# Paged ring, sums in dead blocks and parted VectorE operations in a Strassen kernel for a gated pooling and convolution block

## The chip, the cores and the metric

One core of a Trainium2 chip runs the whole kernel. The metric is the device time of one execution in microseconds (us); the kernel before has a median of 2375.99 us over three runs.

## The reference

A decoder block on x of 256 tokens by 4096 channels, float32. Nearly all of its work is in the projections.

```
h = rmsnorm(x, norm_w)
proj = einsum('bsd,de->bse', h, w_in)              # 4096 -> 20480
u_p, z_p, u_c, b_c, c_c, z_c, g_logit = split(proj)
y_pool = causal_multiscale_pool(u_p, pool_w, pool_scale) * silu(z_p)
y_conv = causal_gated_shortconv(u_c, b_c, c_c, conv_w, conv_b) * silu(z_c)
br = einsum('bsnc,ncd->bsnd', stack([y_pool, y_conv]), w_branch)   # 2048 -> 4096, twice
merged = sum(sigmoid(g_logit + gate_b) * br)
x = x + einsum('bsd,de->bse', merged, w_out)       # 4096 -> 4096
out = rmsnorm(x, final_norm_w)
```

The pool means windows of 2, 4, 8 and 16 tokens by group and maps each group by a 512 x 512 matrix; the convolution has three taps.

## The kernel before, in words

**Units and steps.** An output block of 256 tokens by 1024 columns is a unit. In order: cu0, cc0, cz0, cb0 and cu1 to cb1 (convolution branch, `conv_units`, line 687), pz0, pu0, pz1, pu1 (pool branch), eight gates g0_0, g1_0 to g1_3, eight branch units b0_0, b1_0 to b1_3, four output units o0 to o3. A unit sums over its contraction in steps of 256 rows: 16 steps, in the b units 8. Each step reads one raw weight block of 128 partitions by 2048 numbers, 1 MB.

**Three products.** A number is split into a high part that float32r holds and a low rest, and a product of two is high*high + high*low + low*high: three matmuls of 128 x 128 by 128 x 512. A plain step (P) is eight products, 24 matmuls. A Strassen step (S, Winograd's form) is seven, 21 matmuls, but it needs sums of the weight block's quarters q0 to q3 (`Step.micros`, line 254): T1 and T3 = q0 + q1 and q0 + q2 in V, then V's first half + q2, and that + q3, in W. Of the activations the operands stand in `arena` with their splits, some in Strassen form.

**Who does what.** SyncE loads raw blocks, three buffers in turn (`issue_load`, line 1189). ScalarE copies a piece into the ring as float32r (`act`, line 68), VectorE subtracts to get the low part (`sub`, line 80). TensorE multiplies from the ring (`multiply`, line 1287). All VectorE operations on two tensors have the helper's line 72, all ScalarE ones 69, all step matmuls 1292. Some sums are helped: SyncE loads q0 twice into E, and GpSimd's queue adds q1 and q2 by an accumulating DMA (`move_add`, line 93), so that VectorE has no V to make; `HELPED` (line 624) lists the steps.

**The ring.** 62 pieces of 256 numbers a partition (`Ring`, line 205). A step takes contiguous blocks: 8 and 8 for P, 12, 8 and 8 for S; a block that does not fit before the end goes to the start. Space is given back in the order of its taking.

**What sets the order.** Each engine's instructions keep the order in which the program puts them in. `pump` (line 1214) runs after each group of matmuls: it puts in the next load when the block three before is split (`split`, set in `direct`, line 302), and the preparation of steps up to three ahead while the ring has room. `tick` (line 1280) runs once in six matmuls and takes an item of the unit's epilogue from `queue`, then a phase of a fill (`pop_fill`, line 959). Fills make the operands of the b and o units from y_d and m_d in device memory (stages sa, sb and, for a time, Y), in the last x unit g1_3, the first b units and o0. A Strassen operand's fill is four sums on VectorE (`sums_s`), a split on ScalarE (arena<-sa) and one on VectorE. Unit ends evacuate banks (E<-sums, `evacuate`, line 446). `PLACES` and `OUT` (lines 625 and 855) say which steps of a unit are S; pz1 and g0_0 hold also the band and mixing steps of the pool (`insert`, line 1006).

Of the kernel before, what the change touches and what calls it, by code (L numbers as in the profile page):

```python
# [42 lines left out]
NP_X, NS_X = 7, 9  # L43
NB = 2
NP_Y, NS_Y = (6, 5), (2, 3)
RING = 62
# [5 lines left out]
PACE = 5  # L52
TAIL = 3
# [3 lines left out]
def hybrid_block(ctx: ExitStack, tc: tile.TileContext, x, x_t, norm_t, w_first, w_in, pool_w, pool_scale,  # L57
# [48 lines left out]
    ring = sb("ring", [P, RING * KB], F32R)  # L106
# [4 lines left out]
    W = sb("W", [P, 2, NH])  # L111
# [7 lines left out]
    ossq = sb("ossq", [P, 2, 6])  # L119

# [48 lines left out]
    diag, ones, std = (op.tile([P, P], F32, name=n) for n in ("diag", "ones", "std"))  # L169
    rbc = op.tile([P, T], F32, name="rbc")  # L170
# [20 lines left out]
    class Operand:  # L191


        def __init__(self, kind, view, region):
            self.kind, self.view, self.region = kind, view, region
            self.ready = False

        def block(self, part, i):

            return self.view[:, part, i]  # L200
# [4 lines left out]
    class Ring:  # L205


        def __init__(self, size):
            self.size, self.head, self.live = size, 0, []

        def alloc(self, n):
            at = self.head if self.head + n <= self.size else 0
            for a, m, _, _ in self.live:
                if at < a + m and a < at + n:
                    return None
            if at == 0 and self.head + n > self.size and any(a >= self.head for a, *_ in self.live):
                return None
            block = [at, n, 0, n]
            self.live.append(block)
            self.head = at + n  # L220
            return block

        def release(self, block, n):
            block[2] += n
            while self.live and self.live[0][2]:
                first = self.live[0]
                first[0] += first[2]
                first[1] -= first[2]
                first[2] = 0
                if first[1]:  # L230
                    break
                self.live.pop(0)

    rg = Ring(RING)

    def piece(block, off, n):
        o = (block[0] + off) * KB
        return ring[:, o:o + n * KB]


    def place_of_sum(i):

        return (E, R)[i // 2][:, i % 2].rearrange("p (i n) -> p i n", i=2)


    class Step:
# [7 lines left out]
        def micros(self):  # L254
# [3 lines left out]
            def half(n):  # L258
                def f(block):
                    self.blocks[n] = block  # L260
                    self.h[n] = piece(block, 0, 4).rearrange("p (k n) -> p k n", k=2)
                    self.l[n] = piece(block, 4, 4).rearrange("p (k n) -> p k n", k=2)
                    q = r.rearrange("p (k n) -> p k n", k=2)[:, :, n * NH:(n + 1) * NH]
                    if self is steps[0] and n == 0:

                        act(self.h[n][:, 0], q[:, 0])
                        x_direct(0)
                        for k in range(2):
                            if k:
                                act(self.h[n][:, k], q[:, k])  # L270
                            sub(self.l[n][:, k], q[:, k], self.h[n][:, k].bitcast(F32))
                        return
                    if self is steps[0]:
                        for k in range(2):
                            act(self.h[n][:, k], q[:, k])
                            sub(self.l[n][:, k], q[:, k], self.h[n][:, k].bitcast(F32))
                        return
                    act(self.h[n], q)
                    sub(self.l[n], q, self.h[n].bitcast(F32))
                return f  # L280

            if self.kind == "P":
                self.blocks, self.h, self.l = [None] * 2, [None] * 2, [None] * 2
                return self.pre + [(8, None, half(0)), (8, None, half(1))] + self.post
            if self.kind == "S":
# [5 lines left out]
                def sums(_):  # L291
                    add(V, q[:, 0:1].to_broadcast([P, 2, NH]), q[:, 1:3])
# [1292 lines left out]
```

## Time and profile before

| what | value |
|---|---|
| runs, median (lowest to highest) | 2375.99 us (2373.97 to 2376.92), n 3 |
| profiled execution, first to last instruction | 2371.9 us |
| TensorE busy, matmuls | 2353.5 us, 10483 records |
| VectorE busy, instructions | 2176.7 us, 2234 |
| ScalarE busy, instructions | 1419.7 us, 1474 |
| DMA | 605.60 MB, mean 255 GB/s |
| granted TensorE clock | 0.999 |

The profiled execution has no time of its own beside the span; what lies around its first and last instruction is in the runs' times only. Times in rows are us from the span's start. A row of the order of time gives start, duration, engine, line, operation, out<-in and count; rows of equal work that follow each other are merged, and in brackets stands how long the engine was idle before, and for whom. A matmul's row is 0.39 us long though the next one starts sooner, since they are pipelined. A row of waits gives the waiting engine, the one waited for, the total in us, how often, and the longest. A row of groups gives count, busy us, mean ns of one, then the idle time before.

### The profile page before, as it was taken

To read this page: it belongs to the slowest core of one execution; us is meant where nothing else is said; L and a number is where in the kernel's file an instruction comes from. 1 tells how busy PE (TensorE), PEld (TensorE's weight loads), DVE (VectorE), ACT (ScalarE), POOL (GpSimd) and SP (SyncE) were. 2 spreads that over 40 slices of the span, in tenths; PEclk is the share of its full clock that TensorE was granted. 3 is DMA by queue.
4 is the path that set the end of the run, shared out by engine and by line. 5 is a ranking of instruction groups with operands and counts; after the bars stand their busy time and mean duration, and the time that the engine had idled before them with its cause. 6 is when DMAs were issued, how large, how long until landed. Compare 5 with 4: busy or idle time off the path is not lost.

```text
span 2371.9 us, 28071 instructions
## 1 busy us (share of the span) xinstructions
PE 2353.5 (99%) x10483; PEld 1946.2 (82%) x10483; DVE 2176.7 (92%) x2234; ACT 1419.7 (60%) x1474; POOL 134.5 (6%) x201
## 2 busy tenths in 40 slices
PE   9999999999999999999999999999999999999998
PEld 7888888888888888888888888887878888878886
DVE  8999899989999989989999999988998898899898
ACT  7565565656555656566665656565664556566564
POOL 0000000000002001000000000001100001000000
PEclk9999999999999999999999999999999999999999
DMA  8578678886778658658887888789866667778867
GB/s 335 189 253 252 224 263 276 261 253 215 262 252 265 224 211 251 231 219 262 278 281 232 295 285 276 244 285 293 285 240 226 260 229 267 244 241 285 280 222 267
DMA packets 105257, 605.60 MB, mean 255 GB/s; under 512 B 11232, under 2 KB 11488, under 8 KB 43936
## 3 DMA queue, kind: packets, MB, share of 16 engines
q1 hardware_dynamic: 83216, 512.30, 59.5%
q0 software_dynamic: 21472, 90.45, 16.0%
q8 instruction: 82, 1.34, 0.2%
q10 hardware_dynamic: 432, 1.07, 0.1%
q14 instruction: 55, 0.45, 0.1%
HBM read 571.26 MB, written 25.17 MB: 251 GB/s over the span
## 4 chain that ended last, share of the span: by engine, by line
PE 90%; DVE 5%; DMA 2%; issue 2%; ACT 1%; SPq 0%; POOL 0%; DVEq 0%; ACTq 0%; POOLq 0%
PE sums L1292 66%; PE shared L1292 22%; DVE ring L72 2%; PE shared L804 1%; PE shared L528 1%; DVE W L72 1%; ACT ring L69 1%; DMA R<-in_gate_b_dram 1%; DMA E<-in_w_in_dram 1%; DVE R L72 0%; DMA raw<-in_w_in_dram 0%; DVE V L72 0%; DVE arena L72 0%; DMA raw<-in_w_out_dram 0%; DVE sa L72 0%
## 5 line engine op out<-in xcount | busy, mean ns | idle before, releaser
L1292 PE MATMUL sums<-ring,arena 128*128 128x512 f32 x7641 | 1806.5, 390 | 2.8 <-ACT E L69 2.4
L1292 PEld LDWEIGHTS sums<-ring,arena 128*128 128x128 f32 x7641 | 1431.6, 188 | 301.1 <-ACT E L69 3.3
L72 DVE TENSOR_TENSOR ring<-raw,ring 128x1024 fp32r<-128x1024 f32 (+2 forms) x695 | 942.4, 1382 | 101.8 <-ACT ring L69 97.7
L69 ACT ACTIVATE ring<-raw 128x1024 fp32r<-128x1024 f32 (+2 forms) x695 | 801.8, 1182 | 284.9 <-PE sums L1292 174.9
L1292 PE MATMUL shared<-ring,arena 128*128 128x512 f32 x2484 | 627.7, 389 | 3.6 <-DVE ring L72 3.6
L1292 PEld LDWEIGHTS shared<-ring,arena 128*128 128x128 f32 x2484 | 465.5, 188 | 102.9 <-DVE ring L72 6.0
L69 ACT ACTIVATE ring<-W 128x1024 fp32r<-128x1024 f32 x207 | 219.9, 1062 | 364.2 <-DVE W L72 302.9
L72 DVE TENSOR_TENSOR ring<-W,ring 128x1024 fp32r<-128x1024 f32 x207 | 253.9, 1226 | 23.1 <-ACT ring L69 11.8
L69 ACT ACTIVATE ring<-V 128x1024 fp32r<-128x1024 f32 x154 | 162.7, 1057 | 144.5 <-DVE V L72 119.9
L72 DVE TENSOR_TENSOR V<-raw 128x1024 f32<-128x1024 f32 x154 | 187.9, 1220 | 7.6 <-DMA raw<-in_w_in_dram 6.8
L72 DVE TENSOR_TENSOR ring<-V,ring 128x1024 fp32r<-128x1024 f32 x154 | 187.9, 1220 | 1.3 <-ACT ring L69 1.3
L72 DVE TENSOR_TENSOR W<-W,raw 128x512 f32<-128x512 f32 x207 | 141.9, 685 | 0.0
L72 DVE TENSOR_TENSOR W<-V,raw 128x512 f32<-128x512 f32 x154 | 106.6, 692 | 4.7
L94 POOL DMA_DIRECT2D E<-in_w_in_dram x47 | 41.1, 875 | 765.1 <-DMA E<-in_w_in_dram 322.7
L72 DVE TENSOR_TENSOR R<-R,E 128x1024 f32<-128x1024 f32 (+1 forms) x49 | 77.1, 1592 | 4.0 <-DMA R<-in_gate_b_dram 1.8
L72 DVE TENSOR_TENSOR ring<-E,ring 128x1024 fp32r<-128x1024 f32 x57 | 69.5, 1219 | 1.9 <-ACT ring L69 1.9
L69 ACT ACTIVATE ring<-E 128x1024 fp32r<-128x1024 f32 x57 | 59.7, 1047 | 6.7 <-PE sums L1292 3.7
L72 DVE TENSOR_TENSOR R<-R,shared 128x512 f32<-128x512 f32 x87 | 59.6, 685 | 2.7 <-ACT R L69 0.8
L69 ACT ACTIVATE arena<-sa 128x512 fp32r<-128x512 f32 (+2 forms) x48 | 25.2, 555 | 57.5 <-DVE sa L72 57.5
L69 ACT ACTIVATE E<-sums,rin 128x512 f32<-128x512 f32 x76 | 49.2, 682 | 15.7 <-PE sums L1292 15.7
L72 DVE TENSOR_TENSOR W<-E,raw 128x512 f32<-128x512 f32 x53 | 36.6, 691 | 12.8 <-issue 5.7
L72 DVE TENSOR_TENSOR arena<-sa,arena 128x512 fp32r<-128x512 f32 (+2 forms) x48 | 27.5, 600 | 3.5 <-ACT arena L69 3.5
(143 smaller groups left out, 560.0 us busy)
## 6 DMA issues: line engine op xcount, KB each, us to landing
raw<-in_w_in_dram SPq DMA_DIRECT2D x318, 1024.0 KB, 5.5
raw<-in_w_branch_dram SPq DMA_DIRECT2D x64, 1024.0 KB, 5.2
raw<-in_w_out_dram SPq DMA_DIRECT2D x64, 1024.0 KB, 5.9
E<-in_w_in_dram SPq DMA_DIRECT2D x47, 512.0 KB, 7.3
E<-in_w_in_dram POOLq DMA_DIRECT2D x47, 512.0 KB, 8.6
gates_d<-R POOLq DMA_DIRECT2D x8, 1024.0 KB, 12.0
R<-in_gate_b_dram POOLq DMA_DIRECT2D x7, 1024.0 KB, 12.0
R<-E POOLq DMA_DIRECT2D x4, 1024.0 KB, 9.4
```

Source lines behind the costliest of these rows:

```text
L69: return pin(nc.scalar.activation(dst, src, func, **kw))
L72: return pin(nc.vector.tensor_tensor(out=dst, in0=a, in1=b, op=op))
L94: return pin(nc.gpsimd.dma_start(dst, src, accum_op=ALU.add))
L528: pin(nc.tensor.transpose(shared(j)[:, i * T + t * P:i * T + (t + 1) * P], src[:, t, c:c + P], ident))
L804: pin(nc.tensor.matmul(o, a[:, k, ts], b[:, k], start=(k, i) == (0, 0), stop=(k, i) == (3, 2)))
L1292: pin(nc.tensor.matmul(ps, lhs, rhs, start=n == 0, stop=n == u.total[b] - 1))
```

## The change

**Pages.** The ring is 16 pages of 4 pieces (64 pieces), one page for a high and a low part of 512 numbers. A step takes single pages in circular order, P 2 and 2, S 3, 2 and 2; each page is given back by itself after its product. A piece that crosses the ring's end is split by two instructions on each engine (`parts_of`). In plain steps the matmuls of a bank come in threes, first row block first, instead of sixes.

**Sums over dead raw blocks.** W is gone. The third and fourth sums are written over q0 and q1 of the raw block itself, and the block counts as split only after their own split. That last split is put off (`late`): ScalarE's half is put in between the next step's first copy and VectorE's operation, VectorE's half after the next step's first VectorE operation.

```
@@ Step.micros, kind S
+                    if not helped:
+                        late_high()
+                        add(V, q[:, 0:1].to_broadcast([P, 2, NH]), q[:, 1:3])
+                        self.third = bool(late)
+                        late_low()
+                    else:
+                        self.third = True
+                    if self.third:
+                        add(q[:, 0], v[:, 0], q[:, 2])
...
-                    act(self.dh, q[:, 1:4])
-                    add(W[:, 0], v[:, 0], q[:, 2])
-                    sub(self.dl, q[:, 1:4], self.dh.bitcast(F32))
-                    add(W[:, 1], W[:, 0], q[:, 3])
-                    self.split = True
+                    split(block, q[:, 1:4])
+                    if not self.third:
+                        add(q[:, 0], v[:, 0], q[:, 2])
...
-                    act(self.h13, v)
-                    sub(self.l13, v, self.h13.bitcast(F32))
-                    self.summed = True
+                    split(block, v)
+                    add(q[:, 1], q[:, 0], q[:, 3])
+                    self.summed = now[0]
...
-                    act(self.h24, W)
-                    sub(self.l24, W, self.h24.bitcast(F32))
+                    def low_part():
+                        split_sub(block, q[:, 0:2])
+                        self.split = True
+                    late.append([self, lambda: split_act(block, q[:, 0:2]), low_part])
@@ new
+    def split(block, src):
+        split_act(block, src)
+        late_high()
+        split_sub(block, src)
+        late_low()
```

On VectorE, in o0, where its first two Strassen steps are prepared; V and W hold sums, E gates, Y the branch's part, raw a weight block. Before:

```order
L72 TENSOR_TENSOR R<-R,Y 128x1024
L72 TENSOR_TENSOR V<-raw 128x1024
L72 TENSOR_TENSOR W<-V,raw 128x512
L72 TENSOR_TENSOR ring<-raw,ring 128x3x512
L72 TENSOR_TENSOR W<-W,raw 128x512
L72 TENSOR_TENSOR ring<-V,ring 128x2x512
L72 TENSOR_TENSOR ring<-W,ring 128x2x512
L72 TENSOR_TENSOR V<-raw 128x1024
```

VectorE at the same place of the changed kernel, from the first Strassen step on:

```order
L75 TENSOR_TENSOR V<-raw 128x1024
L75 TENSOR_TENSOR ring<-raw,ring 128x3x512
L75 TENSOR_TENSOR raw<-V,raw 128x512
L75 TENSOR_TENSOR ring<-V,ring 128x2x512
L75 TENSOR_TENSOR raw<-raw 128x512
L75 TENSOR_TENSOR R<-R,E 128x1024
L75 TENSOR_TENSOR R<-R,Y 128x1024
L75 TENSOR_TENSOR R<-R,E 128x1024
L75 TENSOR_TENSOR R<-R,Y 128x1024
L75 TENSOR_TENSOR ring<-raw,ring 128x2x512
L75 TENSOR_TENSOR V<-raw 128x1024
```

No sum stands directly behind the one that it reads now. The last split (ring<-raw,ring 128x2x512), by which the raw block comes free, stands behind the four R operations of the merge, which stood ahead of the step before.

**The sequences.** `SEQUENCES` writes every unit's order by hand, 204 S steps in place of 207, among them:

```
-        "pz1": (3, 6, 8, 9, 10, 11, 12, 14, 15),
+ 'pz1': 'ppbpmmpssppssssppss'
-        "g1_3": (3, 6, 7, 9, 11, 13, 14),
+ 'g1_3': 'ppspspppspsspssp', 'b0': 'ppppppss', 'o0': 'pppppssssppspsps'
```

Before, b0 was PPPPPSPS and o0 PPPPPPSSPSSSPSPS. Two more x operands get Strassen forms, in a tile `more` that lives from g0_0 to the end of g0_3 (`room_for_more`). At the end of b0_0, VectorE before; sa<-sa are a fill's sums, arena<-sa and arena<-Y splits of fills:

```order
L72 TENSOR_TENSOR ring<-V,ring 128x2x512
L72 TENSOR_TENSOR ring<-W,ring 128x2x512
L72 TENSOR_TENSOR ring<-raw,ring 128x1024
L72 TENSOR_TENSOR arena<-Y,arena 128x512
L72 TENSOR_TENSOR ring<-raw,ring 128x1024 x2
L72 TENSOR_TENSOR sa<-sa 128x128 x4
L72 TENSOR_TENSOR ring<-raw,ring 128x1024
L72 TENSOR_TENSOR arena<-sa,arena 128x512
```

VectorE there in the changed kernel:

```order
L75 TENSOR_TENSOR ring<-V,ring 128x2x512
L75 TENSOR_TENSOR raw<-raw 128x512
L75 TENSOR_TENSOR arena<-Y,arena 128x512
L75 TENSOR_TENSOR ring<-raw,ring 128x2x512 x3
L75 TENSOR_TENSOR sa<-sa 128x128 x4
L75 TENSOR_TENSOR ring<-raw,ring 128x2x512 x2
L75 TENSOR_TENSOR arena<-sa,arena 128x512
```

One split of a plain half-step has moved from before the fill's sums to behind them.

**More places for helped sums.** E and R have two each, and the fill's stage sa is a fifth while no fill uses it. `HELPED` is gone: any Strassen step may be helped, if a place is free when its load is two to five loads ahead (`LATEST` 2, `LEAD` 5; before 0 and 3). A helped step loads only q1 to q3 of its raw block. 68 steps are helped in place of 53.

```
-            if helped and helped[0].host is running[0] and sums_from[0] is not None and now[0] >= sums_from[0] and (
-                    helped[0].load_index < state["nl"] + LEAD):
+            if helped and helped[0].load_index < state["nl"] + LEAD:
                 t = helped[0]
-                at = next((i for i in t.slots if sums_in[i] is None or sums_in[i].summed), None)
+                at = next((i for i in t.slots if (in_sa(t) if i == 4 else t.host is running[0] and
+                           sums_from[i // 2] is not None and now[0] >= sums_from[i // 2])
+                           and (sums_in[i] is None or sums_in[i].summed and now[0] >= sums_in[i].summed + SETTLED)), None)
+        elif s.slot is not None:
+            load(r[:, NH:4 * NH], s.src.rearrange("p k n -> p (k n)")[:, NH:4 * NH])
@@ Fill.fetch
-            move(flat(st), self.src)
+            load(flat(st), self.src)
```

The last pair of lines moves the fills' fetches from GpSimd's queue to SyncE's. GpSimd's queue in g1_3 before; 128x1024 into E are the adding DMAs:

```order
L94 DMA E<-in_w_in_dram 128x1024
L91 DMA sb<-y_d 128x512
L94 DMA E<-in_w_in_dram 128x1024
L91 DMA sa<-y_d 128x512
L91 DMA gates_d<-R 128x2048
L91 DMA Y<-y_d 128x512
L91 DMA sb<-y_d 128x512
```

SyncE's queue there in the changed kernel, where 128x2x512 into E is the first half of a helped sum:

```order
L90 DMA sb<-y_d 128x512
L90 DMA raw<-in_w_in_dram 128x2048
L90 DMA E<-in_w_in_dram 128x2x512 x2
L90 DMA sa<-y_d 128x512
L90 DMA raw<-in_w_in_dram 128x2048
L90 DMA Y<-y_d 128x512
L90 DMA sb<-y_d 128x512
L90 DMA raw<-in_w_in_dram 128x2048 x2
L90 DMA sa<-y_d 128x512
L90 DMA Y<-y_d 128x512
L90 DMA raw<-in_w_in_dram 128x1536 x2
```

The fetches of y_d stand between weight loads now, and the halves of both sums are asked for with three loads still before the two raw blocks (128x1536) that they belong to.

390 lines of the change are left out of this document (202 added, 188 removed), and 17 rows, old and new, of the table PLACES.

## The prediction

> **What bounds the kernel now.** I read the page's head first, then the tensor engine's waits, then the order of time at the places where it waited.
>
> ```profile
> span 2371.9 us, 28071 instructions
> PE 2353.5 (99%) x10483; PEld 1946.2 (82%) x10483; DVE 2176.7 (92%) x2234; ACT 1419.7 (60%) x1474; POOL 134.5 (6%) x201
> PE shared L1292 <- DVE ring L72: 3.6, 4, 1.3
> PE sums L1292 <- ACT E L69: 2.4, 2, 2.1
> PE shared L1059 <- DVE rout L1064: 1.1, 1, 1.1
> PE sums L1292 <- DVE ring L72: 0.4, 2, 0.2
> ```
>
> The second line says that the matmuls fill the span; the waits, in all 7.5 us, are the whole of what a better order could win, and 1.1 of them belong to the start. A busy tensor engine could still be a slow one, so I took its pace from rows of merged matmuls:
>
> ```profile
> 1715.35 8.32 PE L1292 MATMUL sums<-ring,arena 128*128 128x512 f32 x36
> 1723.51 2.88 PE L1292 MATMUL shared<-ring,arena 128*128 128x512 f32 x12
> 1728.47 4.83 PE L1292 MATMUL sums<-ring,arena 128*128 128x512 f32 x20 [2.08 <-ACT E L69]
> 1725.95 1.04 ACT L69 ACTIVATE arena<-sa 128x512 fp32r<-128x512 f32 x2 [2.72 <-DVE sa L72]
> 1726.90 1.04 ACT L69 ACTIVATE ring<-raw 128x1024 fp32r<-128x1024 f32 x1
> 1727.85 1.56 ACT L69 ACTIVATE E<-sums 128x512 f32<-128x512 f32 x3
> ```
>
> Thirty-six matmuls take 8.32 us and twelve take 2.88: (8.32 - 2.88) / 24 = 0.2267 us each, whichever step they belong to. So time is the count of matmuls times 0.2267, plus waits. The wait shown is the passage from b0_0 to b1_0: the twelfth matmul of the second row starts at 1723.51 + 11 x 0.2267 = 1726.00, the next at 1728.47, so 2.47 - 0.23 = 2.2 us are lost. Its cause stands on ScalarE: the bank's evacuation (E<-sums) stood behind a fill's split (arena<-sa), which waited 2.72 us for VectorE. The same reckoning at the other places:
>
> ```profile
> 927.30 2.43 PE L1292 MATMUL sums<-ring,arena 128*128 128x512 f32 x10
> 929.97 0.74 PE L1292 MATMUL sums<-ring,arena 128*128 128x512 f32 x2 [0.24 <-DVE ring L72]
> 1645.49 0.39 PE L1292 MATMUL shared<-ring,arena 128*128 128x512 f32 x1
> 1647.17 0.73 PE L1292 MATMUL shared<-ring,arena 128*128 128x512 f32 x2 [1.30 <-DVE ring L72]
> 1649.13 0.39 PE L1292 MATMUL shared<-ring,arena 128*128 128x512 f32 x1
> 1649.98 2.11 PE L1292 MATMUL shared<-ring,arena 128*128 128x512 f32 x8 [0.47 <-DVE ring L72]
> 2087.57 0.50 PE L1292 MATMUL shared<-ring,arena 128*128 128x512 f32 x1
> 2089.37 0.72 PE L1292 MATMUL shared<-ring,arena 128*128 128x512 f32 x2 [1.29 <-DVE ring L72]
> 2091.32 0.40 PE L1292 MATMUL shared<-ring,arena 128*128 128x512 f32 x1
> 2092.24 2.12 PE L1292 MATMUL shared<-ring,arena 128*128 128x512 f32 x8 [0.53 <-DVE ring L72]
> ```
>
> From start to start less 0.23: pz1 loses 0.4 at 929 (929.97 less 927.30 + 9 x 0.2267, less 0.23); g1_3 loses 1.45 + 0.62, with some 0.3 in the longer rows, 2.4; o0 loses 1.57 + 0.69 and some 0.2, 2.5. With the 2.2 above that is 7.5 us in four places. In all but one, VectorE's split into the ring came last. Its load by stage:
>
> ```profile
> 1113.00:1193.90 80.90, 80.90 (x358) 67.00 (x357) 76.31 (x72) 50.17 (x48) 4.90 (x6) 1.00 0.79 258
> 1598.50:1683.40 84.90, 83.14 (x364) 67.78 (x364) 73.99 (x82) 48.98 (x53) 10.43 (x16) 1.00 0.87 285
> 2028.40:2115.30 86.90, 85.08 (x381) 69.57 (x380) 78.83 (x101) 52.49 (x64) 3.18 (x4) 1.00 0.72 233
> ```
>
> After a stretch's length come the busy times of the tensor engine, its weight loads, VectorE, ScalarE and GpSimd, then clock, DMA share and GB/s. The tensor engine works 80.90 of 80.90 us in g1_0, but 83.14 of 84.90 in g1_3 and 85.08 of 86.90 in o0. VectorE is no fuller in the two stages that lose time; it was held up there itself, and ran late. The granted clock is 1.00 in all three.
>
> **The change part by part.** The sequences put 204 Strassen steps where 207 were. Such a step is 21 matmuls, a plain one 24: 9 more, 9 x 0.2267 = **+2.0 us**, on the path with nothing to hide them. The new order inside plain steps (three matmuls on a bank, then the next) costs nothing: Strassen groups of three already run at 0.2267.
>
> VectorE next:
>
> ```profile
> L72 DVE TENSOR_TENSOR ring<-raw,ring 128x1536 fp32r<-128x1536 f32 x207 | 363.2, 1755 | 24.4 <-ACT ring L69 22.5 <-PE sums L1292 0.7
> L72 DVE TENSOR_TENSOR ring<-W,ring 128x1024 fp32r<-128x1024 f32 x207 | 253.9, 1226 | 23.1 <-ACT ring L69 11.8
> L72 DVE TENSOR_TENSOR V<-raw 128x1024 f32<-128x1024 f32 x154 | 187.9, 1220 | 7.6 <-DMA raw<-in_w_in_dram 6.8 <-DMA raw<-in_w_out_dram 0.8
> L72 DVE TENSOR_TENSOR W<-W,raw 128x512 f32<-128x512 f32 x207 | 141.9, 685 | 0.0
> 2047.88 1.22 DVE L72 TENSOR_TENSOR V<-raw 128x1024 f32<-128x1024 f32 x1
> 2049.13 0.69 DVE L72 TENSOR_TENSOR W<-V,raw 128x512 f32<-128x512 f32 x1
> 2049.74 1.75 DVE L72 TENSOR_TENSOR ring<-raw,ring 128x1536 fp32r<-128x1536 f32 x1
> 2051.41 0.69 DVE L72 TENSOR_TENSOR W<-W,raw 128x512 f32<-128x512 f32 x1
> ```
>
> An operation that reads its neighbour's result starts after its end (2049.13 against 2047.88 + 1.22, 0.03 later); one that doesn't starts 0.08 before it (2049.74 against 2049.82). Parting them is worth 0.11 us a pair. A step with its sums on VectorE was 1.22 + 0.69 + 1.755 + 0.685 + 1.22 + 1.226 = 6.8, with the last split waiting for ScalarE's copy of a W just made; I take 0.3 off each of 204, 61 us. Sums made by DMA go from 53 to 68 steps: 15 x 1.22 = 18 off. Three steps from Strassen (6.8) to plain (2 x 1.22): 13 off. Against that, blocks that wrap are split in two (0.685 twice for 1.22, with 0.08 of overlap: 0.08 each, some 60, 5 us), and two more operands get Strassen forms, some 4 us each. Net 61 + 18 + 13 - 5 - 8 = 79, 3 to 4% of 2176.7. None of that is time of the kernel: VectorE is covered by the ring's lead except at the four places.
>
> The Trainium skill speaks against this part: its page "VectorE: DVE Perf Modes", section "The DRAIN you can't avoid", has the next operation wait until the pipe is empty, whether or not a semaphore stands between. By it parting wins nothing and 61 us leave the sum above. The rows here disagree, since independent neighbours overlap by 0.08; no run has yet shown the parted order.
>
> At the places:
>
> - g1_3, 2.4 us lost. What held VectorE:
>
> ```profile
> 1623.12 0.87 POOL L94 DMA_DIRECT2D E<-in_w_in_dram  x1 [8.69 <-DMA E<-in_w_in_dram]
> 1623.66 0.89 POOL L91 DMA_DIRECT2D sb<-y_d  x1
> 1632.64 0.69 DVE L72 TENSOR_TENSOR W<-E,raw 128x512 f32<-128x512 f32 x1 [5.73 <-issue]
> ```
>
> The adding DMA left at 1623.12 and VectorE stood 5.73 us for its sum. The profile names no releaser for that wait; the sum in E is what the operation reads, and its DMA was the last to be issued. A sum is now asked for two to five loads ahead instead of none to three; fills of the operands leave by SyncE's queue, no longer behind the 8.69 us in which GpSimd's stood. Two loads earlier is two steps, 42 x 0.2267 = 9.5 us at least, over the 5.73. I take off 1.9 and leave 0.5 (bounds: 0 to 2.4 left). The page "DMA: Bandwidth & Descriptors" of the Trainium skill, section "Issuing engines are not separate DMA queues", says that another issuing engine saves only issue time; by it the move to SyncE brings nothing, and the earlier request alone would have to do it.
> - b0_0, 2.2 lost. The fill's sums are now put in twelve matmuls ahead of that evacuation, not nine: 3 x 0.2267 = 0.7 us earlier. VectorE has one split of 1.22 fewer in front of them, and 0.3 less in each of two steps: 2.5 us in all. The fill's split still stands before the evacuation on ScalarE, and the sums run late by whatever VectorE lags; I take off 1.8 (bounds 0 to 2.2).
> - pz1, 0.4 lost: one Strassen step fewer there, 6.8 - 2.4 = 4.4 us of VectorE against 0.7 of matmuls. Gone: 0.4 off.
> - o0, 2.5 lost. Four Strassen steps now stand in a row (places 6 to 9) among the same fills and the merge's four R operations of 1.22. Four times VectorE's 6.5 against 21 x 0.2267 = 4.76 eats 7 us of its lead, and the R operations 4 x 1.22; before, they came in twos and threes between plain ones. I add 0.6 (bounds: 2.5 off to 3 more).
> - Elsewhere: what the raw blocks' longer life costs, next. I add 0.4 (bounds 0 to 8).
>
> A raw block used to be free after the second sum. Now sums are written into it, and it is free after the last split, which itself stands behind the next step's first operation: 1.22 + 1.22 + 1.22 - 3 x 0.08 = 3.4 us later, on SyncE's queue, where later loads and now fills stand behind the waiting one.
>
> ```profile
> SPq L87 <- DVE W L72: 1006.4, 207, 11.3
> raw<-in_w_in_dram SPq DMA_DIRECT2D x318, 1024.0 KB, 5.5
> ACT ring L69 <- DMA raw<-in_w_in_dram: 24.9, 20, 3.5
> raw<-in_w_in_dram SPq DMA_DIRECT2D x12, 1024.0 KB, 8.4
> ```
>
> The first row is SyncE's waiting for the old release, once for each Strassen step. So 204 loads go 3.4 us later and land 5.5 after (second row; the last row is the same in g1_3 alone, 8.4), and already 20 times ScalarE waited for one. What hides it: three blocks take turns, so a block comes round in three steps of matmuls, 3 x (204 x 21 + 243 x 24) / 447 x 0.2267 = 15.4 us, in which it is held some 6.5 and loading 5.5, 12 together.
>
> **Sum:** 2376.0 + 2.0 - 1.9 - 1.8 - 0.4 + 0.6 + 0.4 = **2374.9**. The profiled span is 2371.9, 4.1 under the median of the runs, 2376.0; the differences are taken to be the same in both.
>
> **Rivals.** *All waits go* (faster): the four places run dry nowhere, -7.5 + 2.0: 2370.5. For it, VectorE's 79 us; against it, the fills and the row of four in o0. *Late loads* (slower): the 3.4 us reach the tensor engine wherever a step's split is ready less than that ahead of its matmul. The trace has such places in pz1, g1_3 and o0, where the engine ran dry; four or five of them at 2 us are 8 to 10 us over the forecast, some 2384. It decides once holding and loading exceed the cycle: with g1_3's load, 6.5 + 8.4 = 14.9 against 15.4, and against 14.3 where three Strassen steps follow each other. For it, the 20 waits; against it, that a plain step holds its block only 2.4 us, and that a step whose sum DMA made loads three quarters of a block. *Parting does nothing*: 61 us stay on VectorE, only the DMA sums help; g1_3 and pz1 are mended, b0_0 is left at half its 2.2, and o0 loses 2 more: 2376.0 + 2.0 - 1.9 - 0.4 - 1.1 + 2.0 = 2376.6.
>
> **How the numbers follow.** A measurement of this kernel tells 0.2%, 4.75 us, from no change. Forecast 0.36 (own range 2372 to 2379.5) and parting without effect 0.14 lie within it: same 0.50. All waits gone 0.26: faster, since 2370.5 is under 2371.2. Late loads 0.24: slower. The range takes in the first of these and most of the second, 2369.8 to 2384.
>
> **What would show it.** Right: matmuls still 0.2267 apart, 9 more of them; VectorE's busy time near 2100; its waits for DMA sums gone around 1630; loads from SyncE waiting on a ring split instead of W. Wrong: tensor engine waits above 10 us, with ScalarE's waits for raw DMAs well over the 24.9; or waits under 2, with o0 dry nowhere.

## The result, and the profile after

The changed kernel takes 2413.53 us (median of four runs, 2410.4 to 2417.2), the kernel before 2375.93 on the same chip: ratio 1.0163, 95% interval 1.015 to 1.0175, so 1.6% slower, 38 us. The forecast was 2374.9, and the range ended at 2384.

The head of the changed kernel's page:

```profile
span 2410.4 us, 27882 instructions
PE 2366.7 (98%) x10492; PEld 1947.6 (81%) x10492; DVE 2140.1 (89%) x2306; ACT 1414.8 (59%) x1556; POOL 128.4 (5%) x185
```

What its tensor engine waited for (us in all, times, longest):

```profile
PE shared L1306 <- DVE ring L75: 15.3, 18, 1.5
PE sums L1306 <- ACT E L72: 9.7, 7, 2.8
PE shared L1306 <- ACT ring L72: 2.8, 3, 1.2
PE shared L1306 <- DVE R L75: 2.7, 2, 2.0
```

Nine matmuls more, as forecast, but VectorE works less (2140 against 2177 us) and the tensor engine waits for it 18 times where it waited 4. An engine that is less busy and later is itself kept waiting. These waits, above 10 us in all, are the prediction's own sign of being wrong, and so is the next view. What ScalarE, which makes the first half of every split, waited for in the changed kernel:

```profile
ACT ring L72 <- DVE raw L75: 318.0, 146, 8.1
ACT ring L72 <- DMA raw<-in_w_in_dram: 236.5, 117, 6.1
ACT ring L72 <- DMA raw<-in_w_branch_dram: 50.9, 30, 7.3
ACT ring L72 <- DMA raw<-in_w_out_dram: 35.8, 22, 3.8
```

The second to fourth rows are 323 us in 169 waits for raw blocks to be loaded; of before the prediction showed the second row's counterpart, 24.9 us in 20. The chain of work that ended last, by engine, before and after:

```profile
PE 90%; DVE 5%; DMA 2%; issue 2%; ACT 1%; SPq 0%; POOL 0%; DVEq 0%; ACTq 0%; POOLq 0%
```

```profile
PE 63%; DVE 18%; DMA 12%; ACT 3%; issue 3%; ACTq 0%; SPq 0%; DVEq 0%
```

Before, it is the tensor engine's own work; after, 30% of it runs through VectorE and transfers. Where: the stages g0_1, g1_1 and g0_3 (length; busy times of the tensor engine, its weight loads, VectorE, ScalarE, GpSimd; clock, DMA share, GB/s), first in the kernel before, then in the changed one.

```profile
1193.90:1274.80 80.90, 80.90 (x358) 66.99 (x358) 73.53 (x69) 49.34 (x47) 4.38 (x5) 1.00 0.82 270
1274.80:1355.70 80.90, 80.90 (x358) 66.98 (x358) 78.20 (x75) 50.36 (x49) 4.41 (x5) 1.00 0.85 275
1517.50:1598.50 81.00, 81.00 (x359) 67.08 (x358) 73.53 (x69) 49.55 (x47) 5.00 (x6) 1.00 0.83 273
```

```profile
1206.80:1290.80 84.00, 82.03 (x357) 66.87 (x358) 74.32 (x75) 50.57 (x54) 5.23 (x6) 1.00 0.80 257
1290.80:1377.50 86.70, 82.11 (x358) 66.61 (x357) 73.80 (x72) 49.20 (x49) 6.12 (x7) 1.00 0.86 272
1547.70:1634.50 86.80, 84.23 (x362) 68.61 (x362) 70.73 (x71) 47.86 (x49) 4.40 (x5) 0.98 0.78 257
```

Three to six microseconds longer each, at fewer GB/s, with VectorE busy for about as long or less: it is neither bandwidth nor a full engine. The tensor engine's lost time by stage is the start-to-start distances of consecutive 512-column matmuls less 0.2267, summed (what a stage shows in all three columns is transposes and small matmuls); the third column is the run with the old order, below:

| stage | before | after | old order |
|---|---|---|---|
| cb0 | 0.0 | 4.9 | 0.0 |
| cu1 | 2.0 | 6.6 | 4.3 |
| pz1 | 6.2 | 5.6 | 5.6 |
| g1_0, g0_1, g1_1 | 0.0 | 10.9 | 0.2 |
| g0_2, g1_2, g0_3 | 0.0 | 14.2 | 6.0 |
| g1_3 | 2.6 | 2.0 | 0.5 |
| b0_0 | 2.9 | 2.2 | 0.0 |
| o0 | 4.6 | 2.9 | 2.7 |
| o3 | 0.0 | 4.1 | 1.5 |
| all others | 19.3 | 21.1 | 19.7 |
| sum | 37.6 | 74.5 | 40.4 |

36.9 us more and 2.0 for the nine matmuls are 38.9; the spans differ by 38.5. At the four places named by the prediction the changed kernel lost no more than before. All the loss came elsewhere.

How one such loss comes about, in cb0 of the changed kernel: VectorE, ScalarE and SyncE in three answers of the order of time.

```profile
307.49 1.22 DVE L75 TENSOR_TENSOR V<-raw 128x1024 f32<-128x1024 f32 x1
308.62 1.75 DVE L75 TENSOR_TENSOR ring<-raw,ring 128x1536 fp32r<-128x1536 f32 x1
310.29 0.68 DVE L75 TENSOR_TENSOR raw<-V,raw 128x512 f32<-128x512 f32 x1
310.89 1.22 DVE L75 TENSOR_TENSOR ring<-V,ring 128x1024 fp32r<-128x1024 f32 x1
312.02 0.68 DVE L75 TENSOR_TENSOR raw<-raw 128x512 f32<-128x512 f32 x1
315.38 1.23 DVE L75 TENSOR_TENSOR V<-raw 128x1024 f32<-128x1024 f32 x1 [2.67 <-DMA raw<-in_w_in_dram]
316.52 1.22 DVE L75 TENSOR_TENSOR ring<-raw,ring 128x1024 fp32r<-128x1024 f32 x1
...
312.82 1.06 ACT L72 ACTIVATE ring<-raw 128x1024 fp32r<-128x1024 f32 x1 [2.94 <-DVE raw L75]
...
317.76 0.33 SPq L90 DMA_DIRECT2D raw<-in_w_in_dram  x1
```

The first five rows are one Strassen step; its second late sum is done at 312.70 and ScalarE's copy of both at 313.88. All that is left of the step is one split of 1.22. But that split stands behind the next step's first operation, and that one waits for its block until 315.38: VectorE idles 2.67 us, for 1.50 of them with the split ready to run. It runs at 316.52, and SyncE's next load leaves at 317.76, as soon as it has ended; right behind the copy it would have ended at 315.10, 2.6 us earlier. So a raw block is given back only after the next block has arrived. Mostly that one is there in time: in 32 of the 204 Strassen steps ScalarE or VectorE waits for a load in this stretch. In g1_1 the chain of waits shows what that makes (start, us, what):

```profile
1318.56 2.37 DVE ring L75 x2
1320.94 8.65 DMA raw<-in_w_in_dram
...
1329.70 1.50 ACT ring L72
1331.20 0.02 issue
1331.22 2.91 DVE ring L75 x2
1334.15 6.33 DMA raw<-in_w_in_dram
...
1340.58 1.50 ACT ring L72
1342.10 1.83 DVE ring L75 x2
...
1349.12 10.56 DMA raw<-in_w_in_dram
```

Load, copy, two splits, load: between 1300 and 1385 no matmul lies on the chain. From the first VectorE operation on a Strassen step's block to the issue of the load that reuses the block, three loads on, went 4.23 us before and 8.76 after (means over all Strassen steps, paired in the rows of the trace); from a load's arrival to the first use of it by a Strassen step went 5.3 before, 3.0 after. Of the 8.76 us, 5.74 pass until the second late sum is done (4.16 before) and 3.02 from there to the load (less than 0.1 before). The sum itself ends later, since the split of V and, behind another Strassen step, that step's put-off split now stand ahead of it; and of the 3.0 us VectorE is idle for 0.4 on the mean, so most of it is work.

### The profile page after: what moved, and what is told of

Read it like the earlier page. It is cut to its first block, busy times and chain, and to the rows that moved or that the text cites. A ratio compares the mean times of both kernels' runs of the same rounds, so it can differ in the third digit from the quotient of the medians.

```text
span 2410.4 us, 27882 instructions
## 1 busy us (share of the span) xinstructions
PE 2366.7 (98%) x10492; PEld 1947.6 (81%) x10492; DVE 2140.1 (89%) x2306; ACT 1414.8 (59%) x1556; POOL 128.4 (5%) x185
## 4 chain that ended last, share of the span: by engine, by line
PE 63%; DVE 18%; DMA 12%; ACT 3%; issue 3%; ACTq 0%; SPq 0%; DVEq 0%
PE sums L1306 48%; PE shared L1306 13%; DVE ring L75 12%; DMA raw<-in_w_in_dram 10%; ACT ring L72 3%; DVE raw L75 3%; DMA raw<-in_w_out_dram 2%; DVE R L75 2%; DVE V L75 1%; PE shared L782 1%; PE shared L564 1%; DVE sa L75 0%; DVE arena L75 0%; DMA raw<-in_w_branch_dram 0%; ACT R L72 0%
## 5 line engine op out<-in xcount | busy, mean ns | idle before, releaser
L1306 PE MATMUL sums<-ring,arena 128*128 128x512 f32 x7680 | 1820.1, 390 | 10.9 <-ACT E L72 9.7
L72 ACT ACTIVATE ring<-raw 128x1024 fp32r<-128x1024 f32 (+2 forms) x970 | 1011.2, 1085 | 749.6 <-DVE raw L75 318.0
L75 DVE TENSOR_TENSOR ring<-raw,ring 128x1024 fp32r<-128x1024 f32 (+2 forms) x970 | 1188.4, 1260 | 167.4 <-ACT ring L72 163.8
L72 ACT ACTIVATE ring<-V 128x1024 fp32r<-128x1024 f32 (+1 forms) x147 | 144.3, 988 | 111.7 <-DVE V L75 103.3
L75 DVE TENSOR_TENSOR ring<-V,ring 128x1024 fp32r<-128x1024 f32 (+1 forms) x147 | 166.4, 1138 | 3.3 <-ACT ring L72 3.3
L75 DVE TENSOR_TENSOR raw<-raw 128x512 f32<-128x512 f32 x204 | 139.4, 683 | 0.0
L75 DVE TENSOR_TENSOR raw<-V,raw 128x512 f32<-128x512 f32 x136 | 93.0, 684 | 0.0
L75 DVE TENSOR_TENSOR ring<-E,ring 128x1024 fp32r<-128x1024 f32 (+1 forms) x43 | 50.3, 1173 | 1.1 <-ACT ring L72 1.1
L72 ACT ACTIVATE ring<-E 128x1024 fp32r<-128x1024 f32 (+1 forms) x43 | 43.0, 1004 | 0.0
L75 DVE TENSOR_TENSOR raw<-E,raw 128x512 f32<-128x512 f32 x37 | 25.5, 689 | 12.0 <-DMA raw<-in_w_in_dram 8.1
L75 DVE TENSOR_TENSOR ring<-sa,ring 128x1024 fp32r<-128x1024 f32 x26 | 31.7, 1218 | 0.0
```

The costliest lines, as they stand in the source:

```text
L72: return pin(nc.scalar.activation(dst, src, func, **kw))
L75: return pin(nc.vector.tensor_tensor(out=dst, in0=a, in1=b, op=op))
L1306: pin(nc.tensor.matmul(ps, lhs, rhs, start=n == 0, stop=n == u.total[b] - 1))
```

## Experiments

Theory A: the deferral does it, as in the rows of cb0. Theory B: any longer life of a raw block does it, deferred or not. Theory C: the fills and sum requests in SyncE's queue hold the loads up. All ratios are to the kernel before, run on the same chip.

**The deferral alone taken out.**

```
                     late.append([self, lambda: split_act(block, q[:, 0:2]), low_part])
+                    late_low()
```

> The changed kernel, but the last split of a Strassen step is issued at once in its own step, no longer behind the next step's first operation; the sums are still written over the raw block. Theory A (the deferral ties a raw block's release to the next step's load and ring pages, so that only two steps, not three, cover a load): most of the 38 us go, 2376 to 2390, ScalarE's waits for raw loads fall from 323 us to under 120. Theory B (the block is held too long because the sums live in it, deferred or not): a third of the loss goes, 2398 to 2408. Theory C (fills and requests in SyncE's queue hold the loads up): unchanged, 2408 to 2418.

Measured 2500.09, ratio 1.0531 (1.0514 to 1.0549): none of the theories. ScalarE's and VectorE's waits in it:

```profile
ACT ring L72 <- DVE raw L75: 585.0, 204, 5.6
ACT ring L72 <- DMA raw<-in_w_in_dram: 92.7, 50, 5.5
...
DVE ring L75 <- ACT ring L72: 301.4, 275, 4.3
```

The waits for loads did fall (236.5 to 92.7), but ScalarE's for the late sums rose from 318.0, and VectorE's for ScalarE nearly doubled; in the changed kernel it was:

```profile
DVE ring L75 <- ACT ring L72: 172.2, 161, 5.2
```

In the new order the second late sum comes after the second split, so nothing of the step is left to run while ScalarE copies: ScalarE waits for the sum in all 204 steps, and VectorE for the copy. The new order needs the deferral, and the edit did not take out one thing but swapped it for another. The order had to go as a whole (below).

**An early release inside the new order**, with its control. The late sums get a buffer of their own; it costs one page of the ring.

```
-PAGES = 16
+PAGES = 15
...
+    W = sb("W", [P, 2, NH])
...
-                    add(q[:, 1], q[:, 0], q[:, 3])
+                    add(W[:, 1], W[:, 0], q[:, 3])
+                    self.split = True
...
```

> The changed kernel with the two late sums in a buffer of their own again, so that the raw block is free after the second of them; the deferral stays; the ring pays one page (15 of 16). Theories A and B: loads leave early again, ScalarE's waits for raw loads fall under 80 us, time 2374 to 2385 with a microsecond or more for the page. Theory C: 2405 to 2420.

> The changed kernel with a ring of 15 pages and nothing else: the control of the run with sums of their own. A page is a seventh of a Strassen step, 0.7 us of the lead that VectorE has on the tensor engine. Theories A and B: since release waits for the next step's pages too, 2415 to 2435. Theory C: 2411 to 2416.

Measured 2393.92 (1.0066 to 1.0096) with the early release and 2442.23 (1.027 to 1.03) for the control: at 15 pages the release is worth 48 us, more than the whole loss. A block is in use 5.6 us with it and 8.9 in the control. The edit moves two things besides: DMA makes the sums of 63 steps, 71 in the control, and a helped step's first late sum stands behind a put-off split that is still open. ScalarE's waits for raw loads are 255 + 50 + 43 = 348 us in the control and 108 + 13 + 11 = 132 with the release. Both times were above what theories A and B expected; I had put the page at a microsecond, and in the changed kernel it costs 29.

**A fourth raw block**, paid with two pages.

```
-PAGES = 16
-NRAW = 3
+PAGES = 14
+NRAW = 4
```

> The changed kernel with a fourth raw block, paid with two ring pages (14 of 16); the deferral and the sums over dead blocks stay. Theories A and B: one more step of 5 us covers each load, ScalarE's waits for raw loads fall under 60 us; what is left is the price of two pages, 2378 to 2400. Theory C (queue): the loads still stand behind fills, 2400 to 2415.

Measured 2382.89, ratio 1.0034 (1.0021 to 1.0047): 31 us back in spite of two pages fewer, as theories A and B expected. A block is still in use 9.0 us, but a load now lands 7.4 us ahead of its first use. The chain that ended last is the tensor engine's again, and the wait for loads is all but gone:

```profile
PE 92%; DVE 5%; ACT 1%; issue 1%; DMA 0%; SPq 0%; DVEq 0%; ACTq 0%
```

```profile
ACT ring L72 <- DMA raw<-in_w_in_dram: 33.4, 20, 4.7
```

This and the pair before show that late raw blocks carry most of the loss.

**Fills back on GpSimd's queue.**

```
-            load(flat(st), self.src)
+            move(flat(st), self.src)
```

> The changed kernel with the operands' fills fetched by GpSimd's queue again, nothing else undone. Theory C (fills in SyncE's queue hold the raw loads up): 2385 to 2402. Theories A and B (raw blocks are released late): 2409 to 2418, ScalarE's waits for raw loads still around 320 us.

Measured 2429.17, ratio 1.0222 (1.0207 to 1.0237), 16 us slower than the change and above both expectations. Theory C falls, and the other way round, this part of the change was a gain. In g1_3 the loss by stage rises from 2.0 to 12.3 us; VectorE there stood for one fill alone, and GpSimd's queue shows what that fill (Y<-y_d) had stood behind:

```profile
DVE sa L75 <- DMA Y<-y_d: 10.6, 1, 10.6
```

```profile
1674.32 0.90 POOL L97 DMA_DIRECT2D E<-in_w_in_dram  x1 [7.20 <-DMA E<-in_w_in_dram]
1677.08 0.88 POOL L97 DMA_DIRECT2D E<-in_w_in_dram  x1 [1.86 <-DMA E<-in_w_in_dram]
...
1678.17 0.90 POOL L94 DMA_DIRECT2D Y<-y_d  x1
```

The two adding DMAs waited 7.20 and 1.86 us for the plain ones before them, and the fill behind them could only then leave. The transfers themselves are not what differs: the 31 fetches of operands land a median of 5.7 us after their issue here, and of 6.9 us in the changed kernel.

**The release flag alone, in the kernel before.**

```
                     add(W[:, 1], W[:, 0], q[:, 3])
-                    self.split = True
...
                     sub(self.l24, W, self.h24.bitcast(F32))
+                    self.split = True
```

> The kernel before with one thing of the change alone: a Strassen step's raw block is released after the step's last split instead of after the second sum, 1.22 + 1.23 us of VectorE later; no deferral, no sums in the block. Theory B (life of the block): the tensor engine's waits grow by 10 to 25 us, 2385 to 2400. Theory A (only the tie to the next step's load and ring pages does it): 2375 to 2382.

Measured 2389.6, ratio 1.0057 (1.004 to 1.0073), where B was expected; but the trace says that it isn't B. A block's time in use is 4.33 us, against 4.23 before: a load waits on the chip for the last operation that reads its block, which is still the second sum, and the edit only put the load at a later place in program order. The sums that DMA makes are planned by the count of loads, so they moved too: 57 of them for w_in instead of 47 (63 and 53 in all), and VectorE now stands for them:

```profile
DVE W L72 <- DMA E<-in_w_in_dram: 22.8, 7, 8.6
```

That wait was 1.4 us in the kernel before. I put the 14.8 us down to that change of plan, the only one that I see; the question stayed open, and the next run asks it rightly.

**Late sums over the raw block, in the kernel before**, on top of the edit above. Now the block is read until the last split.

```
-                    add(W[:, 0], v[:, 0], q[:, 2])
+                    add(q[:, 0], v[:, 0], q[:, 2])
...
-                    add(W[:, 1], W[:, 0], q[:, 3])
+                    add(q[:, 1], q[:, 0], q[:, 3])
...
-                    act(self.h24, W)
-                    sub(self.l24, W, self.h24.bitcast(F32))
+                    act(self.h24, q[:, 0:2])
+                    sub(self.l24, q[:, 0:2], self.h24.bitcast(F32))
```

> The kernel before with the late sums written over the raw block, so that its data hold the block to the step's last split; order on every engine as in the run with late release, where the trace showed that the load still waited for the second late sum only (first use to the reusing load 4.33 us against 4.23) and the 14.8 us came from sums and loads put in other places. Here the 2.45 us of life are real, about 6.8 us. Theory B (each microsecond of life is dear): 2396 to 2412, 7 to 22 us above the 2389.6 of that run. If life inside the step is nearly free and only the tie to the next step isn't: 2387 to 2394.

Measured 2403.11, ratio 1.0123 (1.0106 to 1.014), where B was expected. The block is in use 6.81 us, as meant, and against the run before, with the same operations and the same sums by DMA, that costs 13.5 us. ScalarE's wait for loads more than doubles, from 41.3 to

```profile
ACT ring L69 <- DMA raw<-in_w_in_dram: 91.1, 67, 7.0
```

So B has its part too: 2.5 us more life, no deferral, 13.5 us of time. VectorE's wait for the sums that DMA makes rose as well, from 22.8 to 35.8 us, and how the 13.5 divide was not taken apart. They lie at single places, pz1 above all (12.5 us lost, 7.2 in the run before); in the six gate stages from g1_0 to g0_3, where the change lost 25.1, this run loses 1.7.

**The old order on VectorE, all else of the change kept.** Late sums stay over the raw block, which is now held to the end of its own step and no longer.

```
...
                 def direct(block):
-                    split(block, q[:, 1:4])
-                    if not self.third:
-                        add(q[:, 0], v[:, 0], q[:, 2])
+                    split_act(block, q[:, 1:4])
+                    add(q[:, 0], v[:, 0], q[:, 2])
+                    split_sub(block, q[:, 1:4])
+                    add(q[:, 1], q[:, 0], q[:, 3])
...
-                    late.append([self, lambda: split_act(block, q[:, 0:2]), low_part])
+                    split_act(block, q[:, 0:2])
+                    low_part()
```

> The changed kernel with the kernel before's order on VectorE in a Strassen step (first late sum beside the split of three, second behind it, last split at once); the sums still lie over the raw block, which is held to the end of its own step. Theory A: the tie to the next step is gone and ScalarE's copy of the late sums is covered by a split again, 2374 to 2388. Theory B: as the kernel before with late release, 2385 to 2402. If the new order is itself worth much of VectorE's time, above 2402.

Measured 2379.67, ratio 1.002 (1.001 to 1.0029): 34 of the 38 us gone, theory A's number. The edit takes out the deferral and the parting together, so it prices the new order as a whole. What ScalarE waited for and VectorE for ScalarE, and of its page the engines and the chain:

```profile
ACT ring L72 <- DMA raw<-in_w_in_dram: 88.2, 55, 5.1
ACT ring L72 <- DMA raw<-in_w_branch_dram: 20.1, 11, 4.5
...
DVE ring L75 <- ACT ring L72: 118.6, 109, 3.3
```

```profile
PE 2356.7 (99%) x10492; PEld 1947.8 (82%) x10492; DVE 2169.1 (91%) x2306; ACT 1425.6 (60%) x1556; POOL 131.1 (6%) x185
...
PE 83%; DVE 10%; ACT 3%; DMA 2%; issue 2%; SPq 0%; ACTq 0%; DVEq 0%
```

The block's time in use is 6.85 us here, between 4.23 and 8.76. The row of the engines gives the price of the parting too: VectorE works 2169.1 us in the old order and 2140.1 in the new one, with the same 2306 instructions. Parting saves 29 us of an engine that wasn't the bound, and with the deferral that it needs it costs the kernel 34. Even VectorE has lost by it: it waits 172.2 us for ScalarE in the new order and 118.6 in the old one.

**One page fewer, in the kernel before.**

```
-RING = 62
+RING = 58
```

> The kernel before with a ring of 58 units instead of 62, one page less. Theory A (a page cost the changed kernel 29 us because releases wait for the next step's pages): here releases don't, so 2376 to 2382. If a page is simply 0.7 us of lead that any of these kernels needs: 2390 to 2410.

Measured 2384.69, ratio 1.0039 (1.0024 to 1.0054): 9.9 us for a page, between the two expectations. A page is worth much in any of these kernels, and three times as much in the changed one (29 us).

**The old order with 15 pages**, the other control of the early release, on top of the old order.

```
-PAGES = 16
+PAGES = 15
```

> The changed kernel with the kernel before's order on VectorE (last split at once, sums over the raw block) and 15 ring pages. It is the control of the run with sums of their own, which has 15 pages, the new order and an early release and took 2393.9. If the new order's whole cost is the late release, that run has none of it left, and this one, whose blocks are held to the step's end, is no faster: 2392 to 2402. If the deferral also costs lead of its own (pages given out and not filled), this one is faster: 2382 to 2391. A page alone cost the kernel before 9.9 us: 2379.7 + 9.9 = 2389.6.

Measured 2393.11, ratio 1.0073 (1.0056 to 1.0089), the same as 2393.92 with the new order and the early release, and in the first range of the expectation. That alone doesn't say that the late release is the whole cost: a block is in use 6.9 us here and 5.6 there, so the new order, with 1.3 us less life, takes as long as the old one. Against the new order with the same 15 pages and the same 71 sums by DMA (2442.23) the old order is worth 49 us, where it was worth 34 with 16 pages; a page costs it 13.4 us.

**Early release for the steps whose sums DMA made**, in the old order.

```
+                w = V if helped else q[:, 0:2]
...
-                    add(q[:, 1], q[:, 0], q[:, 3])
+                    add(w[:, 1], w[:, 0], q[:, 3])
+                    self.split = helped
...
```

> The changed kernel with the kernel before's order on VectorE, and the late sums of a step whose first sums a DMA made (68 of 204) written into V, which such a step leaves idle, so that its raw block is free after the second of them; the others are held to the end of their step; 16 pages. If the block's life is what the run with the old order still loses (2379.7 against 2374.8), a third of its Strassen steps release 2.4 us earlier: 2372 to 2377. If not, 2378 to 2381.

Measured 2381.18, ratio 1.0029 (1.0019 to 1.0038): no gain over the old order's 2379.67, 0.2 us above what was expected if a block's life is not what that run still loses. The stages moved both ways (g0_3 2.1 to 0.5; cu1 4.3 to 6.3, o3 1.5 to 2.7). With loads that leave earlier the sums are planned at other steps, 61 three-quarter loads of w_in where 64 were, so it is not the release alone that differs, and the run doesn't decide it.

**The old order with four raw blocks and 14 pages**, on top of the old order.

```
-PAGES = 16
-NRAW = 3
+PAGES = 14
+NRAW = 4
```

> The changed kernel with the kernel before's order on VectorE, four raw blocks and 14 pages. With four blocks the late release should cost nothing in either order, so against the same with the new order (2382.9) this shows what the order costs apart from the loads: if nothing, 2379 to 2387; if the deferral loses lead, 2374 to 2378; if parting is worth its saving on VectorE, above 2388.

Measured 2373.45, ratio 0.9994 (0.9985 to 1.0003): the kernel before, within what can be told. Against 2382.89 for the new order with the same blocks and pages, the new order costs 9.4 us even where loads are hardly late. I take the cause to be that two pages are given out and stay empty until three more are free for the next step's split; that was not shown by itself. Another candidate stands in the waits: VectorE waits 182.3 us for ScalarE with the new order and 129.5 with the old one, at four blocks each.

**Rows of Strassen steps broken up** in o0 and o3, in that kernel (entries of one line of `SEQUENCES`).

```
-'o0': 'pppppssssppspsps'
+'o0': 'pppppsspsspspsps'
-'o3': 'pspsspsspssppppp'
+'o3': 'ppspsspsspsspppp'
```

> The run with the old order, four raw blocks and 14 pages (2373.45), and two of its sequences changed with the same numbers of steps: o0 without its four Strassen steps in a row (pppppsspsspspsps), o3 with its first five Strassen steps spread (ppspsspsspsspppp). If rows of Strassen steps are what runs VectorE dry in o0 and o3, the 2.7 and 2.4 us lost there go: 2367.5 to 2371. If the epilogue's R operations ahead of o3 and the fills in o0 do it whatever the row: 2372 to 2375.

Measured 2379.05, ratio 1.0018 (1.0009 to 1.0027), slower than either expectation: o0 loses 4.9 us instead of 2.7, o3 3.8 instead of 2.4. Breaking the rows up did not help. The fills follow the same sequence, so their order moved as well; whether the rows do harm by themselves, and what else runs VectorE dry there, wasn't taken apart.

## Why the prediction was wrong

The step that failed is "Elsewhere: what the raw blocks' longer life costs ... I add 0.4 (bounds 0 to 8)". Measured, the time lost elsewhere is the 36.9 us of lost time plus the 3.6 won at the four places, some 40. Late loads carry most of it: a fourth block takes back 31 in spite of two pages fewer. Some 9.4 us, seen with four blocks, belong to the new order itself; the prediction had put the order's cost beside the loads at nothing. The rival *Late loads* had the mechanism and the sign, with a chance of 0.24, but 8 to 10 us. Three things were wrong in its working.

- **Looking only behind the old release.** I took a block to be held 6.5 us, with 3.4 us more behind the second late sum. The 3.4 were nearly right: the runs show 3.0 there. But a block was in use 4.23 us before, so that they make 7.6, and not 6.5. And I didn't look ahead of the second late sum, which now ends 1.6 us later in the step, since parting puts other splits before it. So it was 8.76. The rival's own line, "once holding and loading exceed the cycle" of 15.4 us, is reached by 8.76 + 6.9, the arrival time in the changed kernel's row below. (Both sides are means, the first of Strassen steps, the second of all; a load still lands 3.0 us ahead of its first use on the mean, so the line is crossed in places.) Nor did I ask what the operation ahead of the last split itself waits for: the next block's arrival and, for a split of three, three pages of the ring. That is the loop shown in cb0 and g1_1, but it isn't what makes the mean: with four blocks, where loads are hardly late, a block is in use 9.0 us all the same.

```profile
raw<-in_w_in_dram SPq DMA_DIRECT2D x254, 1024.0 KB, 6.9
```

I had put in 5.5 from the kernel before. With the old order it is 5.6 again, so it isn't what is loaded; but the release flag alone, with 4.33 us in use, has 6.5, so late releases aren't all of it either.

- **Counting places where the lead was already thin.** I charged 2 us at four or five of them. By the table the loss lies mostly in nine other stages instead (cb0, cu1, the six from g1_0 to g0_3, o3), 2 to 6 us each, of which all but cu1 lost nothing before. I take it that VectorE, 92% busy, has little to win a lost lead back with; that was not shown by itself. It is not the 2.5 us of life alone: the kernel before with late sums over the raw block, in use 6.81 us, lost 1.7 us in those six stages.
- **The cover that a wait has.** "with the last split waiting for ScalarE's copy of a W just made" described the old order's one bad pair. I took the new order for the old one without that pair; the run without the deferral shows that it has a worse one, and that the deferral is what hides it.

The other steps, from the changed kernel and from the old order, where they aren't drowned:

- Nine matmuls, 2.0 us: right. The page counts 10492 matmuls and 10483 before.
- VectorE, 79 us less, busy near 2100: the sign right, 36.6 measured. Parting was put at 61 and is 29 (0.14 a step, not 0.3); the rest was put at 18 and is 7.6 (2176.7 to 2169.1). The Trainium skill's rule weighed there ("VectorE: DVE Perf Modes", section "The DRAIN you can't avoid") would have given parting nothing; but the same section has an operation that is not held start earlier, which the prediction left out. The rows of cb0 go with that: 308.62 starts 0.09 before the operation ahead of it ends, 310.89 starts 0.08 before. That no time was won came true all the same, by another way.
- g1_3, 1.9 off: 0.6 off in the changed kernel, 2.1 in the old order. The step holds; the late loads took most of it back.
- b0_0 to b1_0, 1.8 off: all of the passage gone. What b0_0 still loses in the changed kernel (2.2) lies at its start, at 1719.9. With the old order it loses nothing.
- pz1, 0.4 off: 0.6 off. Right.
- o0, 0.6 added: 1.7 off, the wrong sign. Breaking up the four Strassen steps in a row that I feared made o0 worse in the last run, with the fills moved as well, so whether the row does harm stays open.
- Fills on SyncE: I counted them with the help and, under the raw blocks, with the harm. Moving them back costs 16 us. By the Trainium skill's page "DMA: Bandwidth & Descriptors", section "Issuing engines are not separate DMA queues", another issuing engine saves only issue time. The landing times agree, 6.9 us on SyncE's queue and 5.7 on GpSimd's; the runs' times, 2413.5 and 2429.2, don't: as far as the rows show it, what the move saves is waiting before the issue, behind DMAs of the same queue that wait themselves, such as the 7.20 and 1.86 us shown above.

With the loads cured by a fourth block and the order put back, the time is 2373.45, nine matmuls included. That goes with a small gain from the other terms, as forecast, but it can't be told from the kernel before, and it is without the parting. The rival *Parting does nothing* is answered as well: it does something for VectorE and nothing good for the kernel. What stays open is how the 34 us of the new order split between late loads and the rest: with four blocks and 14 pages the rest is 9.4, and with 16 it wasn't measured. Nor was the tie to the next load parted from the longer life as such. Nor was it taken apart which pieces of the change pay for the longer life in the old order, which costs the kernel before 13.5 us and leaves this one at 2379.67; the fills on SyncE, 16 us in the new order, are the largest that was seen.

## What to carry to other kernels

When an edit moves a buffer's release, add up everything that now stands between the buffer's first use and the release, ahead of the old release as well as behind it; and ask what each of these operations waits for. If one waits for the next load, the release is part of a loop with the loads. Work saved on an engine that doesn't bound the kernel was worth nothing here, and a place where it is asked to run ahead (pages of a ring, raw blocks) can be worth more than all of it: here one page was 10 to 29 us. To test a reordering, put the whole old order back; taking out one half left the other uncovered and cost 87 us more.

## What was not expected of the hardware

After some of the waits the tensor engine's granted clock was halved for three microseconds. Stretches of the changed kernel (columns as above; the clock is the third number from the right):

```profile
348.60:351.60 3.00, 0.28 (x2) 0.00 (x0) 2.96 (x5) 2.66 (x5) 0.00 (x0) 1.00 1.00 407
352.60:355.70 3.10, 3.10 (x9) 2.45 (x8) 2.90 (x2) 2.06 (x3) 0.31 (x1) 0.50 0.68 223
1588.20:1591.50 3.30, 1.68 (x7) 0.86 (x6) 3.11 (x3) 2.05 (x3) 0.00 (x0) 1.00 1.05 245
1591.50:1595.00 3.50, 3.50 (x11) 2.72 (x10) 2.04 (x3) 2.10 (x3) 0.00 (x0) 0.51 1.02 414
```

The first pair follows one wait of 2.9 us, the second two shorter ones in which the engine still worked half the time (1.68 of 3.30); single waits of 2.2 us in the kernel before (at 1728) and of 2.4 and even 2.9 us in the run of 2500 us (at 162 and 365) were followed by nothing, so the length of one wait doesn't settle it. Fourteen matmuls are 0.427 us apart instead of 0.227 in the changed kernel, 2.8 us in all, and 36 in the run of 2500 us: waiting has a surcharge, which a sum of waits leaves out.
